# A hybrid decoder layer on one core: the output projection by token halves, two blocks to a PSUM tile

## The chip, the core and the metric

The kernel runs as one program on one NeuronCore of a Trainium2 chip. Its engines are TensorE (PE; its weight loads are shown as PEld), VectorE (DVE), ScalarE (ACT), GpSimd (POOL) and SyncE (SP), which issues the DMAs. Each engine works through its own queue in order, and semaphores tie the queues together. The metric is the device time of one execution in microseconds. Times within the run are counted from the start of the profiled span.

## The reference

One decoder layer is computed for 512 prompt tokens and 8 sequences of 4 sample tokens, 544 tokens together, with model width 1024. All is fp32. Three sub-layers follow each other, each between two RMS norms and with shift, scale and gate from the conditioning c (adaLN):

```python
h = rmsnorm(x, p['ffn1_norm_pre']) * (1 + sc1) + sh1
x = x + 0.5 * g1 * rmsnorm(swiglu(h, ...), p['ffn1_norm_post'])
h = rmsnorm(x, p['mix_norm_pre']) * (1 + sc2) + sh2
y, state = token_mixer(h, ...)      # ends with: y @ p['w_out']
x = x + g2 * rmsnorm(y, p['mix_norm_post'])
h = rmsnorm(x, p['ffn2_norm_pre']) * (1 + sc3) + sh3
x = x + 0.5 * g3 * rmsnorm(swiglu(h, ...), p['ffn2_norm_post'])
```

The mixer joins a gated DeltaNet branch and a sliding-window attention branch per channel, `y = sigmoid(gate_a) * o_dn + sigmoid(gate_b) * o_sw`, and multiplies by `w_out` (1024 x 1024). That last product and the norms on both sides of it are the place of this change.

## The kernel before

*Layout.* Everything is kept transposed: 128 channels on the partitions, the 544 tokens along the free axis. A tensor of width 1024 is 8 blocks of 128 channels. The tokens are cut into two halves of TH = 272, c = 0 and c = 1.

*Products.* A product keeps fp32 accuracy with three matmuls: both operands are split into a rounded part and the rest (`hi`, `lo` of a weight, `hh`, `hl` of the activations), and `mm3` (L293) issues hi x hh, hi x hl, lo x hh for each k-tile of 128 and each half. One matmul has 272 columns. A *unit* is one weight piece of 512 x 128 (256 KB), four k-tiles: it is loaded to a `raw` buffer by `wload` (L273, SP), and split by `wsplit` (L284): ACT casts `hi` (L270), DVE or POOL subtracts `lo` (L271). There are 4 raw buffers (RAW_BUFS) and 3 pairs of `hi`/`lo` (HL_BUFS). `Feed.run` (L224) goes through the units in order, splits one ahead and loads two ahead. The output block takes two units, kh = 0 and 1.

*PSUM.* The pool `pp` has two tiles `pj` of 128 x 2 x 512 fp32. One tile spans two banks, and `project` (L309) puts token half 0 in the first and half 1 in the second.

*Order.* `Streams` (L145) runs a main generator, which gives the matmuls, and side generators that come due when the main one has advanced by the cost they asked for. The order so made is a first draft; the tile framework then orders each engine's queue by its own model of the program, so that instructions of two units can stand mixed, and adds the semaphore waits.

*The output projection* is in `layer` from L1890 on. w_out's blocks 0 and 1 (`8 - NOUT`) are computed for both halves at once (`use`, L1872). Blocks 2 to 7 are computed by halves (`useh`, L1880): first all six for half 0, then all six for half 1. The split weights of these six stay in the tiles `fhw` and `flw` (`keep`, L1893; 48 pieces of 128 x 128 in each) and are used again for half 1 (`held`). The input is the merged mixer output `osw`, split into `hh`, `hl`; its blocks 4 to 7 come late, so that the kh = 0 units of two blocks are run first (`first + 2`, L1913). Then the mixer's memory is given up and the residual stream `xT` is loaded back from `xsp` (L1926).

After block 7 of a half its *boundary* is spawned (L550): sum of squares over channels on PE (`post_s`), a small rsqrt chain on DVE, broadcast on PE (`post_p`), `residual` (L555: per block a multiply L569 and an add L571 on DVE, a square on ACT, a sum on POOL), again a sum (`pre_s`), rsqrt and broadcast (`pre_p`), and `modulate` (L528: DVE L536, ACT L538, DVE L539), which writes `hh` and `hl` for the second FFN. `turn_x` (L727, L735) transposes the new residual stream for the output (`xnps`). The second FFN starts with five blocks for half 0, each a gate product `pg` and an up product `pu` of two units, then the same five for half 1, and then the rest for both halves.

Of the kernel before, what the change touches and what calls it, by code (L numbers as in the profile page):

```python
# [11 lines left out]
F32R = mybir.dt.float32r  # L12
# [7 lines left out]
P = 128  # L20
# [5 lines left out]
TH = T // 2  # L26
# [20 lines left out]
NDOWN = 7  # L47
NFRONT = 5
ORDER = ('B', 'U0', 'U1', 'K', 'V', 'Q', 'U2', 'G0', 'U3', 'G1', 'G2', 'G3', 'G4', 'G5', 'G6', 'G7')
NOUT = 6  # L50
NACT = 1
FLO = True
DLO = (4,)
# [130 lines left out]
def drain(gen):  # L184

    while True:
        try:
            next(gen)
        except StopIteration as e:
            return e.value  # L190
# [1594 lines left out]
def layer(ctx, tc, a, dbg=None, stop=None):  # L1785
    nc = tc.nc
    L = Layer(ctx, tc, a, dbg)
    L.setup()
    sch, feed = Streams(), Feed(L)
    xsp = L.dr.tile([P, 8, T], F32, name="xsp")  # L1790
    hp = L.pool("hp", 1)
    hh = hp.tile([P, 8, T], F32R, name="hh")
    hl = hp.tile([P, 8, T], F32R, tag="hl", name="hl")
    x = (hh, hl)
    mx = Mixer(L, x)
    mx.sch = sch
    mx.open()
    c1 = ExitStack()
    xp = L.pool("xp", 1, c1)
    L.xT = xp.tile([P, 8, T], F32, name="xT")  # L1800
    tmp = L.pool("tmp", 2, c1)
    sqx = xp.tile([P, T], F32, name="sqx")
    sqd = xp.tile([P, T], F32, name="sqd")
    done = set()

    def hook1(c):
        sch.spawn(L.boundary(sqd, env["d"], 2, 3, tmp, sqx, x, c, done), c)

    env = {"tmp": tmp, "sqd": sqd}
    m1 = feed.add(L.ffn("ffn1", x, env, 0, NDOWN, hook1))  # L1810
    mx.plan(feed)
    with ExitStack() as c2:
        sp = L.pool("sp", 1, c2)
        vw = L.load_vectors(sp)
        L.load_cond(sp)
        L.load_x(sp)
        wa = L.pool("wa2", 24, c2)
        ada0 = L.ada([(1, 0), (0, 0)], wa, False)
        for b in range(8):
            for c in range(2):  # L1820
                L.sumsq(L.xT[:, b, :], sqx, b, tmp, c, nc.vector if b % 2 else None)
            if b % 2:
                next(ada0)
        rms0 = L.rms(sqx, (0, 1), "pre0")
        for i in range(4):
            next(ada0)
            if i == 1:
                with tc.issue_after(L.ada_mm.ins):
                    next(rms0)
                    L.use_vectors(*vw)  # L1830
        with tc.issue_after(L.ada_mm.ins):
            rps = drain(rms0)
        drain(ada0)
        for i in range(4):
            feed.fetch(i)
        for i in range(SPLIT_AHEAD):
            feed.prep(i)
        for h in range(2):
            if h:
                drain(L.ada([(1, h), (0, h)], wa, False))  # L1840
            for b in range(4 * h, 4 * h + 4):
                for c in range(2):
                    drain(L.modulate(rps[c], 0, tmp, x, c, b, b + 1))
    fp = env["fp"] = L.pool("fp", 1, c1)
    wap = L.pool("wap", 3, c1)
    env["d"] = fp.tile([P, 8, T], F32, name="dacc")

    def rest():
        yield 0.0, R_LAT
        nc.sync.dma_start(out=L.cst, in_=a["c_cst"])  # L1850
        for pieces in ([(2, 0), (2, 1), (3, 0), (3, 1)], [(4, 0), (4, 1), (5, 0), (5, 1)],
                       [(6, 0), (6, 1), (7, 0), (7, 1)], [(8, 0), (8, 1)]):
            yield from L.ada(pieces, wap)
        done.add("ada")

    def main():
        sch.spawn(rest(), 2)
        yield from feed.run(m1)
        while not ({0, "ada"} <= done):
            yield 0.5  # L1860
        yield from feed.run(mx.mark0)
        while 1 not in done:
            yield 0.5
        nc.sync.dma_start(out=xsp, in_=L.xT)
        c1.close()
        done.clear()
        yield from mx.run(sch, feed)
        st = {}
        us = []
        bufs = {}  # L1870

        def use(b):  # L1872
            def f(ps):
                dd, sq, t = bufs["d"], bufs["sqd"], bufs["tmp"]
                nc.scalar.copy(out=dd[:, b, :].rearrange("p (a b) -> p a b", a=2), in_=ps[:, :, :TH])
                for c in range(2):
                    L.sumsq(dd[:, b, :], sq, b, t, c)
            return f

        def useh(b, c):  # L1880
            def f(ps):
                dd, sq, t = bufs["d"], bufs["sqd"], bufs["tmp"]
                nc.scalar.copy(out=dd[:, b, c * TH:(c + 1) * TH], in_=ps[:, c, :TH])
                L.sumsq(dd[:, b, :], sq, b, t, c, nc.vector if b == 7 else None)
                if b == 7:
                    sch.spawn(L.boundary(sq, dd, 5, 6, t, bufs["sqx"], x, c, done,
                                         lambda c: sch.spawn(last[0].turn_x(c), 2)), c)
            return f

        wo = a["w_out"][0]  # L1890
        last = []

        def keep(b):  # L1893
            def f(kh):
                if "w" not in bufs:
                    bufs["w"] = [bufs["fp"].tile([P, 8 * NOUT, P], F32R, tag=t, name=t + "w") for t in ("fh", "fl")]
                i = (b - 8 + NOUT) * 8 + 4 * kh
                return [t[:, i:i + 4, :] for t in bufs["w"]]
            return f

        for b in range(8 - NOUT):
            us.append(L.project(wo, b * P, x, use(b)))
        u01 = [us[0][0], us[1][0], us[0][1], us[1][1]]
        mo = feed.add(u01 + [u for b in us[2:] for u in b])
        for c in range(2):
            for b in range(8 - NOUT, 8):
                mo = feed.add(L.project(wo, b * P, x, useh(b, c), cs=(c,), keep=keep(b), held=c > 0))
        first = mo - 2 * 2 * NOUT - 2 * (8 - NOUT)
        for b in range(4):
            while not (mx.merged[b] and mx.merged[8]):  # L1910
                yield 0.5
            L.split(hh[:, b, :], hl[:, b, :], mx.osw[:, b, :])
        yield from feed.run(first + 2)  # L1913
        for b in range(4, 8):
            while not (mx.merged[b] and mx.merged[9]):
                yield 0.5
            L.split(hh[:, b, :], hl[:, b, :], mx.osw[:, b, :])
        while sch.side:
            yield 0.5
        mx.c_sp.close()  # L1920
        mx.ctx.close()
        if WD:
            L.open_pw(4)
        xp = L.pool("xp2", 1)
        L.xT = xp.tile([P, 8, T], F32, name="xT2")
        nc.sync.dma_start(out=L.xT, in_=xsp)  # L1926
        tmp = L.pool("tmp2", 2)
        bufs.update(tmp=tmp, sqx=xp.tile([P, T], F32, name="sqx2"), sqd=xp.tile([P, T], F32, name="sqd2"))
        fp = bufs["fp"] = L.pool("fp2", 1)
        d = bufs["d"] = fp.tile([P, 8, T], F32, name="dacc2")  # L1930

        last.append(Last(L, tmp, d, bufs["sqd"], hp, fp))
        feed.add(L.ffn("ffn2", x, bufs, NFRONT, NDOWN, lambda c: sch.spawn(last[0].finish(c, last[0].ps), 0), last[0].block))
        yield from feed.run(mo)
        while 0 not in done:
            yield 0.5
        while 1 not in done:
            yield from feed.run(feed.at + 1)
        yield from feed.run()

    sch.run(main())


# [25 lines left out]
```

## Time and profile before

| | |
|---|---|
| time, median of 3 runs | 1605.7 us (1602.64 to 1608.74) |
| the profiled execution's own time | 1608.77 us |
| its span | 1607.0 us |
| TensorE busy | 1537.5 us (96%) |
| VectorE, ScalarE, GpSimd busy | 887.6, 640.1, 305.9 us |
| mean granted TensorE clock | 0.983 |
| output projection, first to last matmul | 1118.8 to 1170.2 us |
| first matmul of the second FFN | 1179.33 us |

The time of an execution is its span and a little around it. A window of the table of windows gives, for one stretch, the busy time of each engine with the count of its instructions, then the granted clock, the mean share of the DMA engines and what they moved. The chain of waits goes back from the last instruction, at each step to what released it; a piece of it shows start, length, engine, line and the tile. Matmuls overlap, so that the time of one (0.29 us) is longer than the distance from one to the next (0.125 us).

### The profile page before, as it was taken

How to read it: one execution, taken by the hardware profiler on the slowest of the kernel's cores; microseconds unless marked ns; L12 is line 12 of the kernel's file. 1: busy time of each engine (PE TensorE's matmuls, PEld its weight loads, DVE VectorE, ACT ScalarE, POOL GpSimd, SP SyncE). 2: the span in 40 equal slices, each digit the busy share in tenths (PEclk: the TensorE clock that was granted, in tenths of full speed). 3: DMA queues.
4: the chain of work that ended last, by engine and by line, in shares of the span. 5: the costliest groups of instructions: out<-in, count | busy, mean ns of one | idle time of the engine just before them, and what ended most of it. 6: DMA issues, size and time to landing. Idle time of an engine off the chain costs nothing.

```text
span 1607.0 us, 33057 instructions
## 1 busy us (share of the span) xinstructions
PE 1537.5 (96%) x12851; PEld 1418.5 (88%) x12851; DVE 887.6 (55%) x2384; ACT 640.1 (40%) x1449; POOL 305.9 (19%) x443
## 2 busy tenths in 40 slices
PE   7999999999998999998999999999979999999996
PEld 4799999999977999997778888889979999999995
DVE  5433322333598787688889568665474332233365
ACT  4322222222445544445575242223556332223363
POOL 2000000000343231231122134131458000000042
PEclk9999999999999999999999899999999999999998
DMA  9554445445655334653113243624515432333353
GB/s 314 169 183 138 153 136 159 147 148 153 190 167 178 100 75 107 165 135 77 45 45 80 77 121 83 167 55 130 158 53 158 115 86 87 94 87 89 83 152 111
DMA packets 316083, 199.69 MB, mean 124 GB/s; under 512 B 37508, under 2 KB 298335, under 8 KB 315638
## 3 DMA queue, kind: packets, MB, share of 16 engines
q1 hardware_dynamic: 315638, 197.46, 43.5%
q8 instruction: 101, 1.65, 0.4%
q14 instruction: 56, 0.46, 0.1%
q0 software_dynamic: 288, 0.11, 0.0%
HBM read 182.08 MB, written 16.36 MB: 123 GB/s over the span
## 4 chain that ended last, share of the span: by engine, by line
PE 77%; DVE 13%; ACT 3%; DMA 2%; issue 2%; POOL 2%; SPq 0%; DVEq 0%; ACTq 0%; POOLq 0%
PE pg L301 16%; PE pu L301 16%; PE pb L301 16%; PE pd L301 14%; PE adaps L467 3%; DVE y L1194 2%; DVE lo L271 2%; ACT hi L270 1%; PE pov L1065 1%; DVE X L1422 1%; PE pgu L301 1%; DVE s L1016 1%; PE psc L1012 1%; PE pkq L1281 1%; DVE xT L571 1%
## 5 line engine op out<-in xcount | busy, mean ns | idle before, releaser
L270 ACT CAST hi<-raw 128x512 fp32r<-128x512 f32 (+2 forms) x502 | 287.9, 581 | 613.1 <-PE pu L301 172.1
L271 DVE TENSOR_TENSOR lo<-raw,hi 128x512 fp32r<-128x512 f32 (+2 forms) x368 | 252.9, 688 | 385.8 <-ACT hi L270 378.7
L301 PE MATMUL pb<-hh,hi 128*128 128x272 f32 (+1 forms) x1008 | 234.9, 303 | 1.4 <-ACT hi L270 0.7
L271 POOL TENSOR_TENSOR lo<-raw,hi 128x512 fp32r<-128x512 f32 (+1 forms) x104 | 140.6, 1356 | 483.1 <-ACT hi L270 460.5
L301 PE MATMUL pb<-hh,lo 128*128 128x272 f32 (+1 forms) x1008 | 227.7, 296 | 1.3 <-POOL lo L271 0.7
L301 PE MATMUL pb<-hl,hi 128*128 128x272 f32 (+1 forms) x1008 | 227.2, 295 | 1.0 <-DVE hl L271 1.0
L301 PEld LDWEIGHTS pb<-hh,hi 128*128 128x128 f32 (+1 forms) x1008 | 164.6, 191 | 12.0 <-issue 6.5
L301 PE MATMUL pd<-fh,hi 128*128 128x272 f32 x704 | 171.3, 290 | 0.0
L301 PE MATMUL pd<-fl,hi 128*128 128x272 f32 x704 | 170.2, 289 | 0.0
L301 PEld LDWEIGHTS pb<-hl,hi 128*128 128x128 f32 (+1 forms) x1008 | 165.0, 190 | 3.6 <-DVE hl L271 1.5
L301 PEld LDWEIGHTS pb<-hh,lo 128*128 128x128 f32 (+1 forms) x1008 | 164.4, 191 | 4.1 <-DVE lo L271 1.4
L301 PE MATMUL pd<-fh,lo 128*128 128x272 f32 x672 | 162.4, 289 | 4.0 <-POOL lo L271 2.2
L301 PE MATMUL pg<-hh,hi 128*128 128x272 f32 x672 | 149.6, 292 | 7.5 <-ACT hh L538 3.6
L301 PE MATMUL pu<-hh,hi 128*128 128x272 f32 x672 | 148.2, 291 | 0.0
L301 PE MATMUL pg<-hl,hi 128*128 128x272 f32 x672 | 147.0, 289 | 0.3 <-DVE hl L539 0.2
L301 PE MATMUL pu<-hl,hi 128*128 128x272 f32 x672 | 146.1, 289 | 0.0
L301 PE MATMUL pu<-hh,lo 128*128 128x272 f32 x672 | 145.3, 288 | 0.7 <-POOL lo L271 0.7
L301 PE MATMUL pg<-hh,lo 128*128 128x272 f32 x672 | 145.6, 288 | 0.0
L301 PEld LDWEIGHTS pd<-fh,hi 128*128 128x128 f32 x704 | 119.9, 188 | 8.6 <-issue 4.2
L301 PEld LDWEIGHTS pg<-hh,hi 128*128 128x128 f32 x672 | 108.8, 189 | 19.6 <-ACT hh L550 5.0
L301 PEld LDWEIGHTS pd<-fl,hi 128*128 128x128 f32 x704 | 120.2, 188 | 0.0
L301 PEld LDWEIGHTS pd<-fh,lo 128*128 128x128 f32 x672 | 114.1, 188 | 5.6 <-POOL lo L271 2.9
(469 smaller groups left out, 2628.6 us busy)
## 6 DMA issues: line engine op xcount, KB each, us to landing
raw<-w_in SPq DMA_DIRECT2D x136, 256.0 KB, 3.2
wa<-w_ada SPq DMA_DIRECT2D x56, 512.0 KB, 4.4
raw<-ffn_w_gate SPq DMA_DIRECT2D x94, 256.0 KB, 2.9
raw<-ffn_w_up SPq DMA_DIRECT2D x94, 256.0 KB, 7.0
raw<-ffn_w_down SPq DMA_DIRECT2D x92, 256.0 KB, 3.0
wb<-w_ada SPq DMA_DIRECT2D x32, 256.0 KB, 5.8
S<-state_delta SPq DMA_DIRECT2D x8, 512.0 KB, 8.0
delta_sample<-S SPq DMA_DIRECT2D x8, 512.0 KB, 3.4
```

What stands on the lines that cost most here:

```text
L270: self.nc.scalar.copy(out=hi, in_=raw)
L271: (eng or self.nc.vector).tensor_tensor(out=lo, in0=raw, in1=hi.bitcast(F32), op=ALU.subtract)
L301: self.nc.tensor.matmul(out=ps[:m, c, :TH], lhsT=a[:r, kt, :m], rhs=b[:r, kx, c * TH:(c + 1) * TH], start=first and i == 0, stop=last and ...
L467: self.ada_mm = nc.tensor.matmul(out=ps[32 * j:32 * j + 32, :], lhsT=self.cT[:, k, :], rhs=was[j], start=k == 0, stop=k == 7, skip_group_c ...
L571: nc.vector.tensor_tensor(out=self.xT[:, b, s], in0=self.xT[:, b, s], in1=t[:, :n], op=ALU.add)
L1012: nc.tensor.matmul(out=ps[:, i * 256:i * 256 + nk], lhsT=self.qT[64 * h:64 * h + 64, 2 * g + i, qb * P:(qb + 1) * P], rhs=self.kd[64 * h:6 ...
L1016: nc.vector.tensor_tensor_reduce(out=s[:, i, :nk], in0=ps[:, i * 256:i * 256 + nk], in1=am[:, lo:], scale=0.125, scalar=-3e38, op0=ALU.add ...
L1065: nc.tensor.matmul(out=po[64 * h:64 * h + 64, :256], lhsT=self.vn[:, c, 64 * g:64 * g + 64], rhs=pTs[kb][:, 2 * h:2 * h + 2, :], start=kb ...
L1194: nc.vector.scalar_tensor_tensor(out=y[:, :CVN], in0=cv[:, i:i + CVN], scalar=w[i], in1=y[:, :CVN], op0=ALU.mult, op1=ALU.add)
L1281: nc.tensor.matmul(out=pv[:, j], lhsT=kq[:, n, 0, c * P:(c + 1) * P], rhs=kq[:, n, :, c * P:(c + 1) * P], start=True, stop=True)
L1422: e.tensor_tensor(out=xs, in0=xs, in1=pv, op=ALU.subtract)
```

## The change

All eight blocks of the projection now go by token halves: half 0 of all blocks, then half 1 of all blocks. Two blocks, 2i and 2i + 1, share one `pj` tile, each with one half of the tokens in one bank. For half 0 the order of units is kh = 0 of blocks 0 to 3, kh = 1 of blocks 0 to 3, and then blocks 4 to 7 with both units each. `first + 4` units of half the size run before the late part of the input. The first five units (EARLY) come before the memory of the kept tiles is free, so that their split weights are not kept: these five are loaded and split a second time for half 1. The other eleven are kept. The adaLN products stay where they were, beside the first FFN.

```diff
-NOUT = 6
+EARLY = 5
...
-        for b in range(8 - NOUT):
-            us.append(L.project(wo, b * P, x, use(b)))
-        u01 = [us[0][0], us[1][0], us[0][1], us[1][1]]
-        mo = feed.add(u01 + [u for b in us[2:] for u in b])
-        for c in range(2):
-            for b in range(8 - NOUT, 8):
-                mo = feed.add(L.project(wo, b * P, x, useh(b, c), cs=(c,), keep=keep(b), held=c > 0))
-        first = mo - 2 * 2 * NOUT - 2 * (8 - NOUT)
+        def use(b, c, ps):
+            dd, sq, t = bufs["d"], bufs["sqd"], bufs["tmp"]
+            nc.scalar.copy(out=dd[:, b, c * TH:(c + 1) * TH], in_=ps)
+            L.sumsq(dd[:, b, :], sq, b, t, c, nc.vector if b == 7 else None)
...
+        def wout(b, c, kh):
+
+            def go(w):
+                if b % 2 == 0 and kh == 0:
+                    held[c, b // 2] = L.pj("pb")
+                ps = held[c, b // 2][:, b % 2, :TH]
+                hi, lo = w
+                for k in range(4):
+                    kx, ts = 4 * kh + k, slice(c * TH, (c + 1) * TH)
+                    for i, (m, t) in enumerate(((hi, hh), (hi, hl), (lo, hh))):
+                        nc.tensor.matmul(out=ps, lhsT=m[:, k, :], rhs=t[:, kx, ts], start=kx + i == 0,
+                                         stop=kx == 7 and i == 2)
...
+                if kh:
+                    use(b, c, ps)
+            early = order.index((b, kh)) < EARLY
+            parts = None if c and not early else [(0, 4, P, 0, P, wo[kh * 512:kh * 512 + 512, b * P:b * P + P])]
+            return Unit(parts, go, pool_lo=b % 2 == 1 and kh == 0, keep=None if early else lambda: keep(b, kh))
+
+        order = [(b, kh) for kh in range(2) for b in range(4)] + [(b, kh) for b in range(4, 8) for kh in range(2)]
+        first = feed.add([])
+        feed.add([wout(b, 0, kh) for b, kh in order])
+        mo = feed.add([wout(b, 1, kh) for b in range(8) for kh in range(2)])
...
-        yield from feed.run(first + 2)
+        yield from feed.run(first + 4)
```

Three places of the queues show what this does to the order.

TensorE before, from the last matmuls of the projection's half 1 (`pb`, with the kept weights `fhw`, `flw`) to the first of the second FFN (`pg`, `pu`):

```order
L301 MATMUL pb<-hl,fhw 128x272
L301 MATMUL pb<-hh,flw 128x272
L366 MATMUL post_s<-ones,sqd_14471 128x64 x3
L727 MATMUL xnps<-ident,xT_14465 128x128 x4
L366 MATMUL pre_s<-ones,sqx_14470 128x64 x3
L727 MATMUL xnps<-ident,xT_14465 128x128 x8
L353 MATMUL post_p<-ident,rms3y 128x128 x2
L355 MATMUL post_p<-ident,rms3y 128x16
L353 MATMUL pre_p<-ident,rms3y 128x128 x2
L355 MATMUL pre_p<-ident,rms3y 128x16
L727 MATMUL xnps<-ident,xT_14465 128x128 x12
L301 MATMUL pg<-hh,hi 128x272
```

The same place now:

```order
L1900 MATMUL pb<-hl,fhw 128x272
L1900 MATMUL pb<-hh,flw 128x272
L353 MATMUL pre_p<-ident,rms3y 128x128 x2
L355 MATMUL pre_p<-ident,rms3y 128x16
L727 MATMUL xnps<-ident,xT_14477 128x128 x4
L366 MATMUL post_s<-ones,sqd_14483 128x64 x3
L301 MATMUL pg<-hh,hi 128x272
L727 MATMUL xnps<-ident,xT_14477 128x128 x4
L301 MATMUL pg<-hl,hi 128x272
```

Half 0's second sum `pre_s` and three groups of transposes `xnps` have moved up, among half 1's matmuls; half 1's broadcast `post_p` has moved down, behind the FFN's first pair of blocks.

TensorE before, where block 5 of half 0 (tile `pb_14662`) gives way to block 6 (`pb_14699`), each in a tile of its own; the word in brackets is what the matmul waits for:

```order
L301 MATMUL pb_14662<-hl_91,fhw_14510 128x272
L301 MATMUL pb_14662<-hh_90,flw_14511 128x272
L301 MATMUL pb_14699<-hh_90,fhw_14510 128x272 [waits Activation_49]
L301 MATMUL pb_14699<-hl_91,fhw_14510 128x272
L301 MATMUL pb_14699<-hh_90,flw_14511 128x272 [waits DVE_49]
```

TensorE now, where block 6 gives way to block 7 in half 0, both in tile `pb_14646`; `pb_14723` is the first tile of half 1 and `hi_14695` the first weight that is loaded a second time:

```order
L1900 MATMUL pb_14646<-hl_91,fhw_14489 128x272
L1900 MATMUL pb_14646<-hh_90,flw_14490 128x272
L1900 MATMUL pb_14723<-hh_90,hi_14695 128x272 [waits Activation_49]
L1900 MATMUL pb_14723<-hl_91,hi_14695 128x272
L1900 MATMUL pb_14646<-hh_90,fhw_14489 128x272 [waits Activation_49]
L1900 MATMUL pb_14646<-hl_91,fhw_14489 128x272
L1900 MATMUL pb_14646<-hh_90,flw_14490 128x272 [waits Pool_49]
```

Block 7's first matmul waits for ACT a second time, after two matmuls of half 1; its weight was split before, so this wait is for the copy of block 6 out of the same tile.

ACT before, from the copy (L1883) of block 3 to that of block 4 of half 0 (`raw` numbers tell the weights apart):

```order
L1883 COPY dacc2_14475<-pb_14588 128x272
L270 CAST fhw_14510<-raw_14677 128x512
L524 ACTIVATE sqt_14618<-dacc2_14475 128x272
L270 CAST fhw_14510<-raw_14697 128x512
L270 CAST fhw_14510<-raw_14714 128x512
L1883 COPY dacc2_14475<-pb_14625 128x272
L524 ACTIVATE sqt_14655<-dacc2_14475 128x272
```

ACT now, from the cast of block 6's first weight (`raw_14608`) to the copy of block 7 in half 0; `hi_14695`, `hi_14717` and `hi_14755` are weights loaded a second time:

```order
L270 CAST fhw_14489<-raw_14608 128x512
L270 CAST fhw_14489<-raw_14624 128x512
L1878 COPY dacc2_14487<-pb_14573 128x272
L270 CAST fhw_14489<-raw_14644 128x512
L524 ACTIVATE sqt_14639<-dacc2_14487 128x272
L270 CAST fhw_14489<-raw_14661 128x512
L270 CAST hi_14695<-raw_14681 128x512
L1878 COPY dacc2_14487<-pb_14646 128x272
L270 CAST hi_14717<-raw_14699 128x512
L524 ACTIVATE sqt_14676<-dacc2_14487 128x272
L270 CAST hi_14755<-raw_14721 128x512
L1878 COPY dacc2_14487<-pb_14646 128x272
```

The copies of blocks 6 and 7 out of `pb_14646` (L1878) now stand behind casts of weights that are loaded again.

## Rows read from the trace of the kernel before

**Rows 1.** The page: busy time, share and count of TensorE; the 40 slices.

```profile
PE 1537.5 (96%) x12851; PEld 1418.5 (88%) x12851; DVE 887.6 (55%) x2384; ACT 640.1 (40%) x1449; POOL 305.9 (19%) x443
...
PE   7999999999998999998999999999979999999996
```

**Rows 2.** Windows: length, busy us and count by engine, PEclk, DMA share, GB/s.

```profile
1118.80:1132.30 13.50, 12.37 (x95) 11.71 (x94) 10.41 (x16) 9.47 (x18) 3.33 (x4) 1.00 0.57 177
1132.30:1150.40 18.10, 18.10 (x145) 18.10 (x145) 2.41 (x3) 9.28 (x20) 11.30 (x12) 1.00 0.80 242
1150.40:1170.20 19.80, 19.64 (x157) 19.22 (x155) 11.91 (x30) 7.77 (x20) 8.71 (x11) 1.00 0.00 1
1170.20:1179.30 9.10, 5.49 (x45) 4.71 (x44) 6.30 (x34) 3.82 (x9) 0.00 (x0) 1.00 0.01 2
1179.30:1192.05 12.75, 8.04 (x53) 6.70 (x53) 12.67 (x24) 9.14 (x19) 7.29 (x7) 1.00 0.23 62
1192.05:1222.30 30.25, 29.48 (x223) 29.04 (x224) 21.23 (x50) 19.88 (x43) 22.55 (x19) 0.94 0.46 122
1222.30:1600.00 377.70, 368.09 (x2926) 365.13 (x2924) 143.61 (x239) 137.75 (x260) 52.05 (x46) 1.00 0.37 104
...
1190.00:1200.00 10.00, 8.16 (x54) 7.97 (x54) 5.71 (x13) 6.21 (x13) 8.83 (x9) 0.83 0.30 81
```

**Rows 3.** Chain of waits, 1123 to 1198: start us, length us, engine, tile, line.

```profile
1123.34 2.85 DMA raw<-w_out
...
1150.69 0.40 ACT dacc L1883
1151.17 0.44 ACT sqt L524
...
1152.19 0.88 PE post_s L366 x6
...
1157.77 0.22 PE post_p L353 x2
1157.99 0.13 PE post_p L355 x2
...
1171.69 0.88 PE post_s L366 x6
1172.58 0.44 PE xnps L727 x4
1173.02 0.63 PE pre_s L366 x6
...
1179.33 0.39 PE pg L301
...
1186.49 0.32 DVE xT L571
...
1187.55 2.28 DVE xT L571 x2
...
1192.05 2.83 PE pg L301 x12
1194.88 1.98 PE pu L301 x12
1196.86 1.52 PE pg L301 x12
```

**Rows 4.** Timeline of SP and of ACT: the reload of xT, the thirteenth weight's cast.

```profile
1128.91 0.34 SPq L1926 DMA_DIRECT2D xT<-xsp  x1
...
1138.16 0.62 ACT L270 CAST fhw<-raw 128x512 fp32r<-128x512 f32 x1 [1.82 <-DMA raw<-w_out]
```

**Rows 5.** Line L1883: the copy of a block's half, min/median/max ns.

```profile
L1883 ACT COPY dacc<-pb x12: 379/385/386, 1135.5 to 1170.3; 128x272 f32<-128x272 f32 x12
```

**Rows 6.** Timeline of DVE: the last low parts of modulate, half 0 and half 1.

```profile
1184.36 2.13 DVE L539 SCALAR_TENSOR_TENSOR hl<-mt,modT,hh 128x272 fp32r<-128x272 f32 x2
...
1217.50 1.42 DVE L539 SCALAR_TENSOR_TENSOR hl<-mt,modT,hh 128x240 fp32r<-128x240 f32 x1
```

More of the change, by code (lines that the diff above doesn't have):

```diff
@@ L1870, in main @@
         bufs = {}
[L1872 to L1875, printed above, removed]
-                for c in range(2):
[L1877 to L1888, printed above, removed]
@@ L1890, in main @@
         wo = a["w_out"][0]
         last = []
[L1893 to L1899, printed above, removed]
-        for b in range(8 - NOUT):
-            us.append(L.project(wo, b * P, x, use(b)))
-        u01 = [us[0][0], us[1][0], us[0][1], us[1][1]]
@@ L1904, in main @@
-        mo = feed.add(u01 + [u for b in us[2:] for u in b])
-        for c in range(2):
-            for b in range(8 - NOUT, 8):
-                mo = feed.add(L.project(wo, b * P, x, useh(b, c), cs=(c,), keep=keep(b), held=c > 0))
-        first = mo - 2 * 2 * NOUT - 2 * (8 - NOUT)
+        kept, held = {}, {}
+        def use(b, c, ps):
+            dd, sq, t = bufs["d"], bufs["sqd"], bufs["tmp"]
+            nc.scalar.copy(out=dd[:, b, c * TH:(c + 1) * TH], in_=ps)
+            L.sumsq(dd[:, b, :], sq, b, t, c, nc.vector if b == 7 else None)
+            if b == 7:
+                sch.spawn(L.boundary(sq, dd, 5, 6, t, bufs["sqx"], x, c, done,
+                                     lambda c: sch.spawn(last[0].turn_x(c), 2)), c)
@@ new lines, in keep @@
+        def keep(b, kh):
+            if "w" not in bufs:
+                bufs["w"] = [bufs["fp"].tile([P, 4 * (16 - EARLY), P], F32R, tag=t, name=t + "w") for t in ("fh", "fl")]
+            i = 4 * (order.index((b, kh)) - EARLY)
+            return [t[:, i:i + 4, :] for t in bufs["w"]]
+        def wout(b, c, kh):
[9 more added lines that the diff above has]
+                                         stop=kx == 7 and i == 2)
+                    if k % 2:
+                        yield 0.7
+                if kh:
[3 more added lines that the diff above has]
+            return Unit(parts, go, pool_lo=b % 2 == 1 and kh == 0, keep=None if early else lambda: keep(b, kh))
```

## The prediction

> **What bounds the kernel now.** I read the page's busy times first, then the slices, then a table of windows over the stage that the diff touches, then the chain of waits through it, and only then single engines. TensorE is busy 96% of the span, and in the slices the lowest digit between the two ends, a 7, is the thirtieth, 1165 to 1205 [rows 1]. The table shows that it is where the change is [rows 2]: the output projection runs from 1118.8 to 1170.2, the second FFN's first token half starts at 1179.3, its second pair of blocks at 1192.05, and its second token half at 1222.3. From there to 1600 TensorE is busy 368 of 378 us, so time won before 1222.3 reaches the end. Of the 103.5 us of these six windows TensorE is idle 10.4 (13.50 - 12.37, then 0.16, 3.6, 4.7, 0.8), and 1.8 more go to a slow clock. That is the whole prize: about 12 us, 0.75% of the run.
>
> The chain shows why [rows 3]. Half 0 of the projection ends at 1150.4. Its boundary (sum of squares, norm, residual, norm, modulate) takes from the copy at 1150.69 to the first matmul at 1179.33, 28.6 us. Half 1 of the projection covers it only to 1170.2, because just six of eight blocks are left for it: 144 matmuls at 0.125 us (145 in 18.10 us [rows 2]).
>
> **The change, part by part.** *What it moves.* Blocks 0 and 1 were computed for both halves at once; now their second halves, 48 matmuls, come after half 0. The matmuls stay 384. So half 0 could end 48 x 0.125 = 6.0 us earlier and half 1 covers 6.0 us more.
>
> *Start, to 1132.3.* The first 96 matmuls are now half 0 of blocks 0 to 3. They wait for the same late merge of heads 4 to 7, which held TensorE 1.1 us [rows 2]. I keep the 13.5 us; bounds are -1.1 and +1.
>
> *The weight feed of half 0.* From there a 256 KB weight serves 12 matmuls, 1.5 us, and block 6's first weight, the thirteenth load, stands in SP's queue behind the reload of xT, as before. It landed at 1138.16, 9.25 us after that reload was issued, when it was first needed only at about 1144 [rows 4]. Now it is needed at 1132.3 + 48 x 0.125 = 1138.3. The cast (0.62) and the low part must follow: I charge 0.4. Five weights no longer fit the kept tile's order and are loaded and split again, which is 1.3 MB in a stretch whose DMA share falls to 0.00 at 1150 [rows 2]; only the first matters. Its raw buffer is freed at about 1139.5, a load takes 2.85 [rows 3], its cast 0.62: 1143.0. In ACT's queue the copy of block 6 stands behind that cast, so it ends at about 1143.4.
>
> *The shared tile.* A new wait appears in the order: the first matmul of an odd block waits for ACT's copy of the even block in the same tile, though it lies in the other half of the tile. There are eight, four in each half. The trace before has no such wait; the nearest row is the copy, 0.385 us [rows 5], started 0.29 after the last matmul of the half [rows 3]. Uncovered, one costs 0.29 + 0.39, about 0.7; covered by other matmuls, nothing; with a cast (0.62) and a square (0.44) ahead of it in ACT's queue, 1.45 on top of no cover. The scheduler places 2 to 7 matmuls of the next tile in front of most. I charge 0.55 at block 5 (no cover), 0.9 at block 7 of half 0 (1143.4 against 1142.2 and two covering matmuls), 4 x 0.35 in half 1. Bounds for the eight: 0 and 11.6.
>
> The Trainium skill's page "PSUM — Partial Sum Buffer" (section "PSUM bank collisions raise a hardware error") says to guard PSUM by bank and quadrant. The two blocks of a tile lie in different banks, so by that rule these waits buy nothing and the sum would be about 2.9 us lower; the order of the changed kernel has them all the same, so I keep mine.
>
> *Half 0 ends* at 1132.3 + 96 x 0.125 + 0.55 + 0.4 + 0.9 = 1146.2; say 1146.4, 4.0 earlier.
>
> *Half 1.* From there stand 190 matmuls (23.8 us), the four waits (1.4), and, inside the stream now, half 0's two sums and its first broadcast (0.88 + 0.63 + 0.35) and three groups of transposes (0.44 each [rows 3]), 3.2 in all: 1146.4 + 28.4 = 1174.8. The chain of half 0 is no longer last here. Before, its second norm waited behind half 1's first sum (1171.69 [rows 3]); now it stands ahead, and pre_p comes right behind the last projection matmul.
>
> *First matmul of the FFN.* The order puts half 1's sum ahead of it. That came 1.5 after half 1's last matmul and took 0.88 [rows 3]: 1174.8 + 2.4 = 1177.2, 2.1 earlier than 1179.33.
>
> *To the second pair of blocks* it was 12.75 us [rows 2]: modulate, whose last low parts ended at 1186.5 [rows 6], then a wait for two blocks of half 1's residual. In the changed order the residual's norm finishes after modulate, not beside it; I add 0.5. So 1190.4 against 1192.05, 1.6 earlier. What follows is matmuls at the same count.
>
> *What is late next.* Half 1's boundary starts at 1174.8 instead of 1170.2, 4.6 later. Its last low part came at 1218.9 [rows 6]; 4.6 later is 1223.5. The FFN's half 1 starts at 1222.3 - 1.6 = 1220.7 and needs it after 24 matmuls of the lower four blocks and some more, at about 1224.8. Nothing is lost, by 1.3 us.
>
> *Sum:* -1.6. The profiled execution is 1608.77 (span 1607.0, 1.8 around it), at the top of the three runs; their median is 1605.7. So 1607.2 on that execution, and 1604.1 on the median, which I predict as 1604.
>
> **Rivals.** (1) *The waits stay hidden and the clock holds.* Half 0 ends at 1144.3, half 1 at 1171.5, the first FFN matmul comes at 1173.9, 5.4 earlier. Before, after 9 us at 60% and 12.75 us at 63% busy, the granted clock was 0.83 around 1195, that is some time at 1.2 GHz; two groups of twelve took 2.83 and 1.98 instead of 1.52 [rows 2, 3], 1.8 lost. If the shorter gap keeps 2.4 GHz, the gain is 7.2: 1598.5. For it: the scheduler fills seven of the eight waits. Against: the idle stretch right before the slow matmuls stays.
> The skill's page "TensorE: Matmul & The Clock Gate" (section "What's actually happening") says that the default state is throttled and activity releases it, which fits the place of those rows; by it alone the 1.8 hangs on how busy 1177 to 1190 becomes.
>
> (2) *Given back at half 1 of the FFN.* Its boundary is 4.6 later with a spare 1.3. If the residual meets more splits on GpSimd (two of its additions took 2.28 us, one alone 0.32 [rows 3]) and loses 3 more, TensorE waits at 1224: no change, 1605.7.
>
> (3) *Slower: the shared tile.* ACT's queue is in order, and the copies of even blocks now stand behind casts that wait for loads and squares that wait for the residual. My charge for waits and feed is 3.25; the gain is gone when they cost 4.9. At 1.45 for each of eight, 11.6, the run is 8.35 - 1.6 = 6.8 longer: 1612.5. For it: block 7 of half 0 has just this. Against: the placed matmuls, and ACT's share of 9.3 in 18.1 us there [rows 2].
>
> **How the numbers follow.** Forecast 0.50 (its own range 1601 to 1608), (1) 0.20, (2) 0.17, (3) 0.13. The range 1597 to 1611 takes in (1) and most of (3). A measurement of this kernel can tell about 0.5%, 8 us. Only (1) with the start's 1.1 us as well passes 1597.7: faster 0.10. Only (3) with a late feed passes 1613.7: slower 0.05. Within: 0.85.
>
> **What would show it.** Right: half 0's sum near 1147.5, the first FFN matmul near 1177, gaps of 0.3 to 0.9 on TensorE before odd blocks, named by ACT's copy, and no gap at the start of the FFN's half 1. Wrong: a first FFN matmul before 1174.5 (rival 1) or after 1180 (rival 3), a gap above 1 us near 1222 (rival 2), or the thirteenth load landing elsewhere than near 1138.

## The result, and the profile after

| kernel | time, median | to before, 95% interval |
|---|---|---|
| before, 8 runs beside it | 1607.1 us (1602.6 to 1615.5) | |
| changed, 8 runs | 1618.7 us (1611.2 to 1620.4) | 1.0061 (1.0041 to 1.0081) |

The change makes the kernel about 10 us slower. The forecast was 1604, in a range of 1597 to 1611: wrong in sign and outside the range. The profiled execution took 1618.69 (span 1616.9), 9.9 more than that of before.

On the noise, since 10 us are 0.6%: in the traces of this study the projection's first matmul comes anywhere from 1109.6 to 1121.0, behind code that no kernel here changes, so I also compare the *stage*, from that matmul to the seventh silu of the second FFN. It is 115.2 us before and 123.4 after; a second trace of before gives 116.7. For before it is counted from 1118.30, not from the 1118.80 of the table and of [rows 2]: the last 384 `pb` matmuls of its trace begin there, at the first product of a k-tile and 0.52 us ahead of ACT's copy `tg`, as in every other trace of this study:

```profile
1118.30 0.41 PE L301 MATMUL pb<-hh,hi 128*128 128x272 f32 x2
```

The page of the changed kernel, TensorE's total and its slices, answers to [rows 1]:

```profile
PE 1539.6 (95%) x12851; PEld 1419.7 (88%) x12851; DVE 896.6 (55%) x2387; ACT 642.8 (40%) x1456; POOL 310.5 (19%) x445
...
PE   7999999999998999998999999999979999999995
```

The same matmuls and the same one 7 at the thirtieth slice: the page doesn't show the loss. The windows do, cut at the changed kernel's own stages; compare [rows 2], whose columns they have:

```profile
1118.18:1127.07 8.89, 7.13 (x53) 6.48 (x52) 7.31 (x11) 5.28 (x10) 1.86 (x2) 1.00 0.50 147
1127.07:1131.75 4.68, 4.58 (x21) 4.26 (x21) 3.23 (x6) 3.10 (x7) 1.58 (x1) 0.64 0.79 221
1131.75:1148.59 16.84, 16.14 (x124) 15.70 (x125) 5.04 (x6) 9.31 (x21) 7.39 (x8) 1.00 0.75 246
1148.59:1178.16 29.57, 28.20 (x220) 27.12 (x220) 16.53 (x43) 13.86 (x32) 15.97 (x17) 1.00 0.23 63
1178.16:1180.81 2.65, 1.69 (x16) 1.49 (x14) 2.26 (x6) 2.52 (x6) 0.00 (x0) 1.00 0.00 0
1180.81:1195.88 15.07, 9.08 (x63) 8.05 (x63) 12.91 (x33) 8.17 (x17) 5.21 (x4) 0.88 0.26 71
1195.88:1230.30 34.42, 30.16 (x226) 29.08 (x224) 25.70 (x55) 20.24 (x45) 23.50 (x21) 0.95 0.41 108
```

The last three rows matter most. The pause between the projection and the FFN shrinks from 9.1 us to 2.65, as intended. But the first pair of FFN blocks takes 15.07 us instead of 12.75, and from the second pair to the FFN's half 1 it is 34.42 instead of 30.25, with TensorE idle 4.3 instead of 0.8. The first rows show two more items: the projection itself now takes 60.0 us (51.9 before, from 1118.30), and in the second window the granted clock is 0.64.

The chain of waits of the changed kernel, with the columns of [rows 3]:

```profile
1174.89 3.28 PE pb L1900 x24
1178.16 0.22 PE pre_p L353 x2
...
1179.95 0.85 PE post_s L366 x6
...
1186.46 1.18 DVE rms3y L340
...
1189.33 1.19 DVE rms3a L343
...
1192.07 0.40 PE post_p L353 x2
...
1195.88 2.72 PE pg L301 x12
...
1205.01 1.27 POOL lo L271
...
1226.66 1.29 DVE ts L548
1227.96 0.39 DVE mt L536
1228.37 0.49 ACT hh L538
...
1229.95 0.30 ACT sil L607
...
1230.30 0.78 PE pg L301 x4
```

Where matmuls overlap other work of TensorE, the chain's times lie a little behind the timeline's: the first FFN matmul starts at 1180.62 there and the second pair at 1195.53. Three things are to be seen. `pre_p` of half 0 runs at 1178.16, right behind the projection's last 24 matmuls. Half 1's `post_p`, 1175.24 before (1.7 us ahead of half 0's `pre_p`), is now at 1192.07, 14 us behind it. And tiny DVE operations stand in the chain with 1.2 us each. GpSimd's and DVE's timelines side by side explain the last:

```profile
1184.89 2.73 POOL L271 TENSOR_TENSOR lo<-raw,hi 128x512 fp32r<-128x512 f32 x2 [8.61 <-ACT hi L270]
1189.23 2.48 POOL L271 TENSOR_TENSOR lo<-raw,hi 128x512 fp32r<-128x512 f32 x2 [1.61 <-ACT hi L270]
```

```profile
1184.65 0.15 DVE L369 TENSOR_SCALAR rmsx<-post_s 128x3 f32<-128x3 f32 x1
...
1186.39 1.25 DVE L340 TENSOR_SCALAR rms3y<-rmsx 128x3 int32<-128x3 int32 x1
...
1189.14 0.16 DVE L345 SCALAR_TENSOR_TENSOR rms3y<-rms3a,rms3y 128x3 f32<-128x3 f32 x1
1189.33 1.18 DVE L343 SCALAR_TENSOR_TENSOR rms3a<-rmsx,rms3y 128x3 f32<-128x3 f32 x1
1190.55 1.18 DVE L344 TENSOR_TENSOR rms3a<-rms3a,rms3y 128x3 f32<-128x3 f32 x1
1191.76 0.16 DVE L345 SCALAR_TENSOR_TENSOR rms3y<-rms3a,rms3y 128x3 f32<-128x3 f32 x1
```

A 128x3 operation takes 0.16 us alone and 1.2 while GpSimd makes a low part, which itself takes about 1.3. The Trainium skill, page "SBUF — State Buffer", section "🔬 SBUF: two separate sides", says that DVE and GpSimd share a pair of ports that is locked for a whole instruction, so that the other one blocks, if the DVE operation has two inputs in SBUF or runs in a 2-port mode. The rows agree: `rms3a<-rms3a,rms3y` ends at 1190.55 + 1.18 = 1191.73, where GpSimd's 1189.23 + 2.48 = 1191.71 ends. `rms3y<-rmsx`, with one tensor input, ends in the same way (1187.64 against 1187.62); in which mode it ran no row shows.

The kernel before has such operations too, for instance in half 1's second norm:

```profile
1203.11 1.28 POOL L271 TENSOR_TENSOR lo<-raw,hi 128x512 fp32r<-128x512 f32 x1 [0.23 <-ACT hi L270]
1205.06 1.28 POOL L271 TENSOR_TENSOR lo<-raw,hi 128x512 fp32r<-128x512 f32 x1 [0.66 <-ACT hi L270]
```

```profile
1203.13 1.28 DVE L344 TENSOR_TENSOR rms3a<-rms3a,rms3y 128x3 f32<-128x3 f32 x1
...
1205.26 0.47 DVE L536 SCALAR_TENSOR_TENSOR mt<-xT,modT,pre_p 128x240 f32<-128x240 f32 x1 [0.30 <-PE pre_p L355]
```

Measured against the shortest run of the same operation in any trace, 14 DVE operations of before lose 10.1 us beside GpSimd from the end of the projection to the FFN's half 1, 2.1 of it in the norm's. In the changed kernel 12 lose 12.6, 5.3 of it in the norm's. The stretching as such is not new; what may be new is that TensorE waits for it.

TensorE's waits from 1178 to 1231, by what was waited for (us in all, times, longest):

```profile
PE post_p L353 <- DVE rms3y L345: 2.8, 1, 2.8
PE xnps L727 <- DVE xT L571: 2.2, 2, 1.5
PE pg L301 <- ACT sil L607: 2.0, 1, 2.0
PE pu L301 <- POOL lo L271: 1.6, 2, 1.1
...
PE pu L301 <- DVE fhx L609: 0.7, 1, 0.7
```

### The profile page after: what moved, and what is told of

It is laid out like the page before. It is cut to its first block, busy times and chain, and to the rows that moved or that the text cites. A ratio compares the mean times of both kernels' runs of the same rounds, so it can differ in the third digit from the quotient of the medians.

```text
span 1616.9 us, 33084 instructions
## 1 busy us (share of the span) xinstructions
PE 1539.6 (95%) x12851; PEld 1419.7 (88%) x12851; DVE 896.6 (55%) x2387; ACT 642.8 (40%) x1456; POOL 310.5 (19%) x445
## 4 chain that ended last, share of the span: by engine, by line
PE 77%; DVE 12%; ACT 3%; issue 3%; DMA 2%; POOL 2%; SPq 0%; DVEq 0%; ACTq 0%; POOLq 0%
PE pg L301 15%; PE pu L301 15%; PE pd L301 14%; PE pb L301 14%; PE adaps L467 3%; PE pb L1900 3%; DVE y L1194 2%; DVE lo L271 1%; PE psu L1661 1%; PE pov L1065 1%; PE pgu L301 1%; PE psc L1012 1%; ACT hi L270 1%; DVE s L1016 1%; PE pkq L1281 1%
## 5 line engine op out<-in xcount | busy, mean ns | idle before, releaser
L270 ACT CAST hi<-raw 128x512 fp32r<-128x512 f32 (+2 forms) x508 | 291.5, 582 | 617.0 <-PE pu L301 171.3
L271 DVE TENSOR_TENSOR lo<-raw,hi 128x512 fp32r<-128x512 f32 (+2 forms) x371 | 256.7, 693 | 388.4 <-ACT hi L270 381.3
L271 POOL TENSOR_TENSOR lo<-raw,hi 128x512 fp32r<-128x512 f32 (+1 forms) x107 | 144.7, 1355 | 492.3 <-ACT hi L270 467.0
L301 PE MATMUL pb<-hh,hi 128*128 128x272 f32 (+1 forms) x976 | 227.8, 302 | 1.3 <-ACT hi L270 0.7
L301 PE MATMUL pb<-hh,lo 128*128 128x272 f32 (+1 forms) x976 | 220.6, 295 | 1.3 <-POOL lo L271 0.7
L301 PE MATMUL pb<-hl,hi 128*128 128x272 f32 (+1 forms) x976 | 219.7, 294 | 0.0
L301 PEld LDWEIGHTS pb<-hh,hi 128*128 128x128 f32 (+1 forms) x976 | 159.0, 190 | 11.7 <-issue 7.4
L301 PEld LDWEIGHTS pb<-hh,lo 128*128 128x128 f32 (+1 forms) x976 | 159.0, 190 | 4.1 <-DVE lo L271 1.4
L301 PEld LDWEIGHTS pb<-hl,hi 128*128 128x128 f32 (+1 forms) x976 | 159.6, 190 | 1.9 <-issue 0.8
```

What stands on the lines that cost most here:

```text
L270: self.nc.scalar.copy(out=hi, in_=raw)
L271: (eng or self.nc.vector).tensor_tensor(out=lo, in0=raw, in1=hi.bitcast(F32), op=ALU.subtract)
L301: self.nc.tensor.matmul(out=ps[:m, c, :TH], lhsT=a[:r, kt, :m], rhs=b[:r, kx, c * TH:(c + 1) * TH], start=first and i == 0, stop=last and ...
```

## The experiments

All were timed beside the kernel before; ratios are to it. "The stage" is the one defined above. Line numbers shift by one to three in the edited kernels.

### The terms of the change, one at a time

**pair_copy.** Each tile is copied once, when both its blocks are done:

```
-            nc.scalar.copy(out=dd[:, b, c * TH:(c + 1) * TH], in_=ps)
+            nc.scalar.copy(out=dd[:, b - 1:b + 1, c * TH:(c + 1) * TH], in_=ps)
...
-                if kh:
+                if kh and b % 2:
...
```

> Edit: ACT copies the two blocks of a tile together, once the odd block is done, so that no matmul waits for a copy out of its own tile. The waits and the two steps behind each took 2.9 us of the changed kernel's projection. Theory T2 (the shared tile is the main cause, my rival 3): nearly all of the 10 us comes back, 1608 to 1611. Theory T1 (half 1's norm stands behind half 0's modulate on DVE, and what follows is pushed on from there): only these 2.9 us come back, the last projection matmul ends near 1175.3, and the time is 1615 to 1617; the gaps after the first FFN matmul stay.

Measured 1616.5 (1.0059, 1.0038 to 1.0080); stage 122.2; the projection 2.4 us shorter. The waits for the copy (1.9 us of waiting in the changed kernel's projection) are gone from TensorE's waits there:

```profile
...
PE pb L1901 <- ACT hh L270: 1.2, 2, 0.6
...
PE pb L1901 <- DVE flw L271: 0.2, 1, 0.2
```

So in the projection the shared tile costs what the prediction charged, 2 to 3 us. Little of it reaches the end: the stage is 1.2 us shorter, and the ratio is nearly the changed kernel's (1.0059 against 1.0061). It isn't the cause of the 10, and T2 falls.

**pre0_ahead.** Half 0's second norm (sum, rsqrt) and `pre_p` are issued with a higher priority:

```
+HPN = (0, 300)
...
-        rp, = yield from self.rms(sqx, (c,), f"pre{seg}")
+        rp, = yield from self.rms(sqx, (c,), f"pre{seg}", HPN[1] if c == 0 and gseg == 5 else 0)
...
+            with self.ahead(hp):
+                self.bcast_cols(r, [(3 * i, 0, P), (3 * i + 1, 0, P), (3 * i + 2, e, P)],
...
```

> Edit: half 0's second norm and its broadcast pre_p get a higher priority in the order, so that pre_p no longer stands behind the last 24 projection matmuls (its rsqrt was ready at 1175.6, it ran at 1178.16). If the first FFN matmul sets the end, as my prediction had it, the first FFN matmul comes 1 to 2 us earlier and the time is 1616.5 to 1618. Theory T1: the second pair waits for half 1's norm (near 1192 to 1195 whatever half 0 does), so at most 0.5 us comes back: 1618 to 1619.

Measured 1612.5 (1.0031, 1.0013 to 1.0050): more than any theory gave it; stage 119.1. `pre_p` now comes 0.2 us after the last rsqrt step, and the first FFN matmul 0.5 after the last of the projection (2.7 in the changed kernel):

```profile
1164.73 0.38 PE L354 MATMUL pre_p<-ident,rms3y 128*128 128x128 f32 x2
...
1168.96 0.37 PE L302 MATMUL pg<-hh,hi 128*128 128x272 f32 x1
```

Its trace also lacks the slow clock at the projection's start (1.5 us in the changed kernel's), so of the 4.3 us of the stage about 2.8 are left for the edit; its interval and the changed kernel's overlap a little.

**post1_first.** Half 0's modulate waits in the draft until half 1's norm is issued, the order of before:

```
+        done.add(("post", c))
...
+        while gseg == 5 and ("post", 1) not in done:
+            yield 0.0, 0.3
         yield from self.modulate(rp, seg, tmp, x, c)
```

> Edit: half 0's modulate is issued only after half 1's norm (sum, rsqrt, broadcast), as the kernel before had it. Theory T1: half 1's broadcast comes near 1184.5 instead of 1192.07, half 0's modulate and the first FFN matmul 4 to 5 us later (near 1185), the second pair of blocks near 1193 and the FFN's half 1 3 to 5 us earlier than 1230.3: 1613.5 to 1616. Theory T4 (only the work of TensorE in this stretch counts, the order of the two boundaries does not): the first FFN matmul's delay is paid in full, 1619 to 1623.

Measured 1618.2 (1.0066, 1.0045 to 1.0088); stage 125.2. The order is what it should be, `post_p` at 1183.34 and the first FFN matmul at 1186.71, yet the second pair comes at 1201.33, not 1193:

```profile
1183.34 0.40 PE post_p L353 x2
...
1186.71 0.60 PE pg L301
...
1201.33 3.08 PE pg L301 x12
```

What half 1's norm wins by its place, half 0 loses, and six runs gain nothing: as the whole cause T1 falls. The trace is no clean price of the order, since the granted clock was 0.55 from 1185 to 1192 in it, where the changed kernel's trace has 1.00.

**turn_late.** The output's transposes begin 30 units later (`yield 0.0, 30.0` at the head of `turn_x`). All instructions are there, but in this order the output gets wrong residual rows, so that its time is a hint only.

> Edit: the transposes of the new residual stream for the output come 30 cost units of the order's draft later, out of the projection and the first FFN pairs. Theory T4 (half 0's 24 transposes and sums were in TensorE's idle time before and are in its stream now): the projection ends 1.4 us earlier, the second pair 3 to 4 us earlier, 1614 to 1616. Theory T1 alone (only the norm's place counts): the order also brings half 1's broadcast forward, ahead of the second half of the first pair, so that 1612 to 1615 fits both; under T2 or under a pure clock cause (T3) nothing changes, 1617.5 to 1620.

Measured 1620.6 (1.0080, 1.0054 to 1.0106), stage 122.7. The second pair comes 12.2 us after the first FFN matmul (1192.27 against 1180.08; 15.07 in the changed kernel), so the transposes do hold it back; but then TensorE is idle 7.4 us from 1200 to 1235 (4.3 in the changed kernel). T4 falls as far as this goes: TensorE's work isn't what limits this stretch.

**before_again**, the kernel before once more:

> The kernel before, word for word, for a second trace of it: how long its stage from the projection's first matmul to the first block of the FFN's half 1 is in another execution (114.7 us from the first projection matmul to the seventh silu of the second FFN in the first trace, 123.4 in the changed kernel's). If the stage is what differs between the kernels, 114 to 116; if the 8.7 us are the chance of one execution (the clock), up to 118.

1609.3 in a single run, stage 116.7, although its clock is low in more places (0.57 from 1172 to 1180). The 7 to 8 us of the stage are no chance of one trace of before.

### Is half 1's boundary short of cover?

**nfront6** (`NFRONT = 6`), **pre0_nf6** (with pre0_ahead) and **pre0_pair_nf6** (with pair_copy too), and then **pre0_pair** with five blocks again:

> Edit: NFRONT 5 to 6, so that six blocks of the FFN's half 0 (instead of five) stand ahead of its half 1, 48 matmuls or 6 us more. Theory T5 (half 1's boundary takes about 50 us from the end of the projection and is no longer covered, since five blocks give 30 us and the 9.4 us of head start are gone): the 3 to 4 us of idle TensorE between 1200 and 1231 go, 1614 to 1616. Theory T1 (the order of the two norms) and T2 (the tile): no change, 1617.5 to 1620.

> Edit: half 0's second norm with a higher priority (which alone gave 1612.5) and NFRONT 6. By T5 the earlier start of the FFN only pays when there is work to cover half 1's boundary: 1608 to 1610. If the earlier pre_p already gave what there was: 1612 to 1613.

> Edit: the two of the run before and the copy of both blocks of a tile at once. The tile's waits (2.9 us in the changed kernel) go as well: 1605 to 1608 by T5 with T2 as a term of 2 to 3 us; if the copy is hidden by now, the same as without it.

> Edit: the second norm of half 0 with a higher priority and the copy of both blocks at once, with five blocks of the FFN's half 0 (NFRONT 5) as in the changed kernel. It says what NFRONT is worth in the run before (1610.85): by T5 (cover) 1613 to 1616; if the cover isn't what is missing, the same, 1610 to 1612, and the stage from the first projection matmul to the seventh silu is 119 to 120 us.

Measured: nfront6 1616.7 (1.0049, 1.0025 to 1.0072), stage 122.9; pre0_nf6 1615.1 (1.0033, 1.0017 to 1.0049), 120.0; pre0_pair_nf6 1610.9 (1.0015, 1.0000 to 1.0029), 119.4; pre0_pair 1611.3 (1.0018, 1.0005 to 1.0030), 119.4. The sixth block is worth nothing that is clear of the noise, and pre0_nf6 lies above both of its expectations. nfront6 has the same waits in the same places as the changed kernel, though half 1's first block isn't next there:

```profile
PE pg L301 <- ACT sil L607: 2.0, 1, 2.0
PE pu L301 <- POOL lo L271: 1.7, 2, 1.2
```

Behind the second pair's start TensorE doesn't wait for half 1's result but for the FFN's own silu and low parts, which stand in the same queues as half 1's boundary. T5 falls.

### What slows the queues

Three edits on pre0_pair_nf6 (1610.9). **sil_ahead**: silu and the product behind it get a higher priority in the half-width blocks. **turn_low**: the transposes get a lower one. **lo_half**: low parts of kh = 1 units on DVE:

```
-                                   pool_lo=len(cs) == 1 and FLO))
+                                   pool_lo=len(cs) == 1 and FLO and kh == 0))
```

> Edit on the kernel with both edits and NFRONT 6: the silu and the product behind it in the FFN's half-width blocks get a higher priority, so that the fifth block's silu stands ahead of two hh activations of half 1's modulate on ACT instead of behind them. T6 (the in-order ACT queue holds the FFN's epilogue behind half 1's modulate): the gap of 1.5 to 2 us ahead of the sixth block's first matmul goes, 1608.5 to 1609.5. If half 1's modulate itself is what is late, the gap only moves to the first block of half 1: 1610 to 1612.

> Edit on the same kernel: the transposes of the residual stream get a lower priority in the order; half 0's then stand between the last projection matmul and the first FFN matmul, as in the kernel before, and half 1's come behind its modulate. T8 (transposes at the head of TensorE's queue wait for the residual and hold the second pair of blocks, 3.1 us): 1607 to 1609. If what counts is half 1's boundary on DVE: 1610 to 1613, since pre_p moves back behind the last projection matmul.

> Edit on the same kernel: of the FFN's half-width blocks only the kh = 0 units make their low parts on GpSimd, the kh = 1 units on DVE. T7 (small DVE operations of half 1's boundary take 1.2 us instead of 0.16 to 0.45 while GpSimd subtracts, 14 us in sum): half of these go, and the time is 1607 to 1611 though DVE has 24 subtractions of 0.69 more. If GpSimd does not matter, DVE is only fuller: 1613 to 1618.

sil_ahead: 1607.6 (1.0002, 0.9989 to 1.0014), stage 117.6. The wait for the silu falls from 1.5 to 0.3, but a wait of 1.7 for the product behind it (`fhx`) appears; the direction fits T6, the gap has mostly moved, and the interval overlaps that of pre0_pair_nf6. turn_low: 1618.7 (1.0067, 1.0051 to 1.0084), stage 125.4, outside both expectations: with the transposes out of the way `pre_s` went behind the last projection matmul (1173.96) and `post_p` to 1192.54; the edit changed the order in more places than its own, and says nothing on T8. lo_half: 1605.5 (0.9985, 0.9973 to 0.9997), stage 115.4: 5.3 us less by one line, and below its expectation of 1607 to 1611. T7 stands, so it was tried alone, with controls and doses.

**after_lo_half**, **before_lo_half**: that line alone, in the changed kernel and in the one before. **after_lo_none**, **before_lo_none**, **lo_none** (on pre0_pair_nf6): `FLO = False`, no low part of these blocks on GpSimd.

> Edit on the changed kernel alone: the kh = 1 units of the FFN's half-width blocks make their low parts on DVE instead of GpSimd; TensorE's order stays the same. T7 (GpSimd's subtractions stretch the DVE operations of half 1's boundary and hold back the FFN's own low parts): of the 4.3 us of idle TensorE between 1200 and 1231 about 3 go, and the wait of 2.8 for post_p shrinks: 1612 to 1615.5. Without T7: 1618 to 1622, as DVE has more to do.

> The control: the same edit on the kernel before. There TensorE is idle 0.8 us after 1200 and half 1's norm runs while GpSimd is idle. If T7 belongs to the change, nothing to win: 1606 to 1610. If it is a general gain that has nothing to do with the change, 4 to 5 us faster: 1602 to 1604.

> One constant in the changed kernel (FLO): no low part of the FFN's half-width blocks is made on GpSimd, all on DVE. With half of them on DVE it took 1611.6 (7 us less). If GpSimd's subtractions are what costs, the rest of the stretched DVE operations (6.2 us) goes too: 1608 to 1612; if DVE's load takes over, 1613 to 1618.

> The control: the same constant in the kernel before. Half of it gave nothing there (1609.4 against 1608.6). T7 as a matter of the change: 1606 to 1611, no gain. If it gains as the changed kernel does, 1601 to 1604.

> The dose: as lo_half (1605.5), but all low parts of the half-width blocks on DVE, none on GpSimd. T7 alone would give up to 4 us more (DVE operations stretched by 6.4 us are left in lo_half); but DVE then has 24 more subtractions of 0.69 us. If DVE's load decides, 1607 to 1613; if the sharing does, 1602 to 1605.

| low parts on GpSimd | all | kh = 0 only | none |
|---|---|---|---|
| changed | 1618.7, 1.0061 | 1611.6, 1.0013 (0.9998 to 1.0027) | 1609.2, 1.0006 (0.9990 to 1.0022) |
| stage | 123.4 | 118.8 | 118.1 |
| pre0_pair_nf6 | 1610.9, 1.0015 | 1605.5, 0.9985 (0.9973 to 0.9997) | 1605.6, 0.9978 (0.9963 to 0.9993) |
| stage | 119.4 | 115.4 | 113.8 |
| before | 1607.1, 1 | 1609.4, 1.0008 (0.9992 to 1.0024) | 1607.8, 1.0000 (0.9981 to 1.0019) |
| stage | 115.2, 116.7 | 117.4 | 116.0 |

(The stages of before are counted from the first of its last 384 `pb` matmuls.) One line takes 7 us from the changed kernel, with intervals apart, and nothing from the one before. after_lo_half has the changed kernel's order of TensorE but for a few neighbours in the first pair, and its windows show where the time comes from; the first row answers to 1180.81:1195.88 above, the second to 1195.88:1230.30:

```profile
1181.61:1195.84 14.23, 9.13 (x65) 8.14 (x65) 12.65 (x36) 8.28 (x17) 2.56 (x2) 0.91 0.27 75
1195.84:1225.84 30.00, 29.77 (x225) 29.33 (x224) 23.05 (x57) 19.65 (x42) 14.44 (x14) 0.93 0.43 116
```

Second pair to half 1: 30.0 us instead of 34.4, at TensorE idle 0.2 instead of 4.3, GpSimd 14.4 instead of 23.5. Its waits:

```profile
PE post_p L353 <- DVE rms3y L345: 2.6, 1, 2.6
PE xnps L727 <- DVE xT L571: 2.2, 2, 1.6
PE post_s L366 <- DVE sqd L525: 1.0, 1, 1.0
PE pg L301 <- DVE hl L539: 0.2, 1, 0.2
PE pu L301 <- POOL lo L271: 0.2, 1, 0.2
```

The waits for the silu (2.0) and the product (0.7) are gone and that for the low parts is 0.2 of 1.6; those for the norm and the transposes stay, against the expectation, by which the wait for `post_p` would shrink. The line does two things at once: it takes GpSimd's subtractions from beside the DVE operations, and it makes these low parts on DVE, in 0.69 us instead of 1.3. Of the 4.1 us of waits that it removes, 1.4 were for a low part itself and 2.7 for the silu and the product behind DVE's chain; no run separates the two. In lo_none the norm's steps beside the FFN's splits are short again:

```profile
1203.60 0.69 DVE L272 TENSOR_TENSOR lo<-raw,hi 128x512 fp32r<-128x512 f32 x1
1204.21 0.16 DVE L341 TENSOR_SCALAR rms3y<-rmsx 128x3 int32<-128x3 int32 x1
```

**best**, lo_half with sil_ahead:

> Candidate: the changed kernel with both blocks of a tile copied at once, half 0's second norm with a higher priority, NFRONT 6, the silu of the half-width blocks with a higher priority, and half of the low parts on DVE. The silu gave 3 us, the low parts 5 us, each on the same kernel; if they add up, 1602 to 1604; if both remove the same gap, 1605 to 1607.

Measured 1607.3 (1.0000, 0.9984 to 1.0015), stage 115.3: nothing beyond lo_half, as if both removed the same gap. The only versions under the kernel before are lo_half and lo_none, by 0.15 and 0.22%, with intervals that just stay below 1. Against before_lo_none, of another batch, lo_none is 2.2 us lower, with overlapping intervals.

## Why the prediction was wrong

*What it got right.* That half 0 ends earlier than the 1150.4 of before; the shared tile: 2.85 charged for its waits, 2.9 found in the changed kernel's projection (waits and the step behind each), 2.4 less projection in pair_copy. Rival 3 named that mechanism as the way to a slower kernel, and it is not the one. The feed charge of 0.4 was not needed: TensorE waits for no weight from 1131.75 to 1148.59.

*The steps, predicted and measured.*

| event | predicted | measured | error added |
|---|---|---|---|
| 97th projection matmul | 1132.3 | 1134.9 | 2.6 |
| half 0 ends | 1146.4 | 1148.6 | -0.4 |
| half 1's last matmul ends | 1174.8 | 1178.2 | 1.2 |
| first FFN matmul | 1177.2 | 1180.8 | 0.2 |
| second pair | 1190.4 | 1195.9 | 1.9 |
| FFN's half 1 | 1220.7 | 1230.3 | 4.1 |
| end of the profiled execution, against before | -1.6 | +9.9 | 1.9 |

The failed step is "what is late next", with its verdict "nothing is lost, by 1.3 us", and the 0.5 added ahead of the second pair. Both took half 1's boundary over from the trace of before with the length that it had there, 1170.2 to 1218.9, and only moved it by 4.6. It now takes 54.9 us instead of 48.7, from 1178.16 to its last low part at 1233.1. Before, its first 9 us ran while the FFN had not begun, with GpSimd at 0.00 and no instruction [rows 2], and its first norm took 3.6 us from the sum (1171.69) to `post_p` (1175.24). Now it starts 2.5 us ahead of the FFN's first matmul, and that norm takes 12.1 (1179.95 to 1192.07): DVE, busy with half 0's modulate, takes the sum up only at 1184.65, and GpSimd, which subtracts from 1184.89 on, stretches three of the norm's operations by 1.0 to 1.1 us each. Later DVE operations of the boundary lose 0.8 to 1.1 us each in the same way. Behind them on ACT stand the hh of half 1, behind these the FFN's silu, and TensorE waits for that at the end of the chain. The losses to GpSimd grew only from 10.1 to 12.6 us. What changed is what they cost: in before TensorE was idle 0.8 us from the second pair to half 1, and taking subtractions from GpSimd bought nothing there. That the lost head start is what exposes them is argued from these rows; no run gives the head start back alone. Rival 2 had the place and even named GpSimd, but only as "no change", worth 3 us; the loss there is 4.1, 6 with the second pair, and in after_lo_half the two windows are 5.3 us shorter again.

The 0.5 ahead of the second pair also rests on a short reading: in before the last wait there, 1.84 us at 1192.05, was for the FFN's silu on ACT and not for half 1's residual.

The second miss is the start, which was to stay as it was, with bounds of -1.1 and +1. The first 96 matmuls took 16.7 us instead of 14.0 (1118.30 to 1132.3 before):

```profile
1134.88 0.28 PE L1900 MATMUL pb<-hh,fhw 128*128 128x272 f32 x1
```

1.5 of these 2.7 are the clock. In the changed kernel three matmuls ran in the 3 us before 1127.07, two of them behind a wait for the late input; then the granted clock was 0.64 over 4.7 us, that is 1.2 GHz for a part of it, and matmuls stood 0.227 us apart instead of 0.126: 1.5 us for 15 of them. Eight of the sixteen traces with the new projection have it and eight don't (pre0_ahead and post1_first among them); the four with the old one don't. No run separates it from the change. Two stages that differ by 1.5 can differ by this alone: lo_half's trace has it and lo_none's hasn't (115.4 and 113.8). The changed kernel's and after_lo_half's both have it.

The order was a third: `pre_p` "right behind the last projection matmul" was read off the order and counted as no loss, while its rsqrt was done 2.6 us earlier (1175.6). pre0_ahead puts it at 2.8 us of the stage; from pair_copy to pre0_pair it is 2.7, of which the clock at the projection's start, low in the first of the two traces only, is up to 1.5. So 1.2 to 2.8.

*What stays open.* after_lo_none still has a stage 1.4 to 2.9 us above before's. pair_copy's 1.2 us and `pre_p`'s 1.2 to 2.8 would account for it; only lo_none has all three edits, and its stage (113.8) is below before's. Between the two things that after_lo_half's line does, the split of its gain is open too. The last 1.9 us, behind the FFN's half 1, stay unexplained.

## What to carry to other kernels

When a change makes two chains run at the same time that ran one after the other, don't carry over a chain's length from the old trace: look up which engines were empty beside it there, and what will run on them now. A short stage with an idle TensorE can be the place where another chain runs at full speed. And before a chain's end is called "right behind" the work ahead of it, ask when its input is ready: in an in-order queue the difference is lost.

## What the runs showed of the hardware

A 128x3 DVE operation of 0.16 us takes 1.2 while GpSimd subtracts 128x512, also one with a single tensor input (`rms3y<-rmsx`, 1.25). An operation that reads PSUM is not held: of the DVE operations that began with over 0.5 us of a subtraction to go, all 8 in before and all 11 in the changed kernel whose tensors lie in SBUF took longer, and none of the 11 and 3 that read PSUM did (`mt<-xT,modT,pre_p` at 1205.26 took its usual 0.47). Moving the subtraction to DVE costs 0.69 each there and was free in this stretch: with half of the subtractions DVE was busy 23.0 us from the second pair to half 1, against 25.7 without them, since its other operations were no longer held. All of them on DVE gave little or nothing beyond half. Outside rival 2 I had priced GpSimd only as an engine with a queue of its own, not as one that stops DVE.
